# Queries, keys and gates of an encoder block's mixer as pairs of tiles by seven block products, with attention operands stored split and bias and masks as one table

## The chip, the cores and the metric

The kernel runs on one core of one Trainium2 chip. The metric is the device time of one execution in microseconds (us), median of several runs. The profile is one execution of the same program, taken by the hardware profiler.

## The reference

One encoder block over 1024 tokens of width 1024, in float32. The parts that matter here are the projection of the mixer and its two branches:

```python
h = h + 0.5 * swiglu(rms_norm(h, ffn1_norm[i]), ffn1_w_gate[i], ffn1_w_up[i], ffn1_w_down[i])
u = rms_norm(h, mix_norm[i])
z = u @ w_in[i]
q, k, v, s_in, gates = jnp.split(z, splits, axis=-1)      # 512, 512, 512, 512, 2048 columns
y_attn = neighbourhood_attention(q, k, v, na_rpb[i]) @ w_attn_out[i]
y_ssm = s5_branch(s_in, ...) @ w_ssm_out[i]
g_attn, g_ssm = jnp.split(jax.nn.sigmoid(gates), N_BRANCH, axis=-1)
h = h + (g_attn * y_attn + g_ssm * y_ssm) @ w_out[i]
h = h + 0.5 * swiglu(rms_norm(h, ffn2_norm[i]), ffn2_w_gate[i], ffn2_w_up[i], ffn2_w_down[i])
h = h + (p[i] @ ple_w_proj[i]) * jax.nn.sigmoid(rms_norm(h, ple_norm[i]) @ ple_w_gate[i])
return rms_norm(h, final_norm)
```

The attention has 8 heads of 64 over a grid of 16 x 64 tokens; each token sees a window of 8 x 16, with a learned bias by relative place. The state-space branch (S5) runs a complex scan forward and backward for 32 groups of 16 channels, adds a skip, applies GELU and then a gated linear unit: `y * sigmoid(y @ glu_w + glu_b)`.

## The kernel before

All large products are in float32 of two parts: an operand x is stored as xh (rounded) and xl = x - xh, and a product is three passes of TensorE (PE) into one bank of PSUM: xh by wh, xl by wh and xh by wl (`mm3`, lines 184 to 186, of 128x128 by 128x512). The helper `split` (lines 152 to 154) makes the two parts, xh by a copy on ScalarE (ACT) and xl by a subtraction on VectorE (DVE).

Both feed-forward stages already compute their matrices by blocks of two by two with seven products in place of eight: `b_operand` makes the weight side of such a product by sums of blocks on DVE, and A7, ACC7 and NEW7 are the lists of the seven activation operands, of the banks that they add to, and of whether a product begins that bank. The mixer before does not: `proj` (L1037) computes one tile of 128 output columns by 512 tokens as 8 products, each of three passes.

PE's program order is the order in which the code is written. The stage of the mixer, from `sin` (the S5 input, at 684 us) to the last gate tile (1168 us), has one main sequence: S5 input, values, then for four pairs of heads q and k, with the 16 gate tiles (`gt`, L1360) among and behind them. Beside it runs a generator, `mixer_side` (L1286): after every three passes `tick` counts down, and when the count is out the generator advances by one piece of work and yields the number of ticks until the next. Its pieces are the normalisation of the tokens' second half, the injection of the S5 inputs into the scan buffer X, the scan on GpSimd (POOL, L1088), 64 units of attention (8 heads, two row halves, four column blocks), the S5 outputs, and the GLU. `drain` empties what is left of the generator at once.

One unit of attention is, in three calls that lag behind one another, scores (two matmuls, bias and mask, exponential), a transposition, and the products with the values. Its operands stand in SBUF: `qk_proj` writes q and k from PSUM split; `load_v` reads a block of v from DRAM and splits it; `make_tabs` adds bias, row masks and column masks on DVE.

The S5 output of one of 16 pairs of groups (`ssm_out`, L1097) loads two matrices and the inputs by SP, copies the states out of X (`xs`, L1111), has 12 small matmuls on PE (`yo`, L1117 and L1119) and stores the result to y_d in DRAM. From unit 48 of the attention on, each unit is followed by one pair. The GLU reads y_d back in another layout (`yt`, 32 DMAs, L1255), applies GELU, splits, loads its weights (`wgs`, L1269) and computes 8 tiles of 4 products (`glu`), with gate products between. Each engine works through its own queue in order, and so does SP, which issues most of the DMAs. What stands behind a waiting DMA there waits too.

Behind the mixer come the branch products (`br`), which read the attention's and the GLU's outputs from DRAM, the product with w_out, the second feed-forward and the embedding.

## Time and profile before

| | |
|---|---|
| time, median of 3 runs | 2099.38 us (2097.23 to 2100.48) |
| span of the profiled execution | 2094.5 us |
| DMA | 285.19 MB moved, 136 GB/s mean over the span |
| HBM | 201.01 MB read, 82.31 MB written |

The profiled execution is one of its own, measured by the span between its first and last instruction; the runs are timed from outside. The page lists busy time for each engine, the chain of work that ended last, and groups of instructions by line. Answers on tiles give duration (least, median and greatest) and first and last start of all instructions with one name; rows of windows give busy times of the engines in a stretch.

### The profile page before, as it was taken

To read this page: it belongs to the slowest core of one execution; us is meant where nothing else is said; L and a number is where in the kernel's file an instruction comes from. 1 tells how busy PE (TensorE), PEld (TensorE's weight loads), DVE (VectorE), ACT (ScalarE), POOL (GpSimd) and SP (SyncE) were. 2 spreads that over 40 slices of the span, in tenths; PEclk is the share of its full clock that TensorE was granted. 3 is DMA by queue.
4 is the path that set the end of the run, shared out by engine and by line. 5 is a ranking of instruction groups with operands and counts; after the bars stand their busy time and mean duration, and the time that the engine had idled before them with its cause. 6 is when DMAs were issued, how large, how long until landed. Compare 5 with 4: busy or idle time off the path is not lost.

```text
span 2094.5 us, 28063 instructions
## 1 busy us (share of the span) xinstructions
PE 2074.5 (99%) x9662; PEld 1705.4 (81%) x9662; DVE 1416.1 (68%) x2420; ACT 999.6 (48%) x1832; POOL 399.4 (19%) x636
## 2 busy tenths in 40 slices
PE   8999999999999999999999999999999999999998
PEld 3788888888888888888898888788888888888886
DVE  7897776667967334677753668995665665786855
ACT  6434333334445333667774635643333334445543
POOL 0037556441000006888200001000000000000000
PEclk9999999999999999999999999999999999999999
DMA  3435444475533551233477745243324238433302
GB/s 134 143 118 154 125 135 120 144 270 169 188 114 111 159 189 64 70 97 98 123 208 260 247 145 117 77 150 121 100 86 135 82 121 297 155 106 94 118 21 81
DMA packets 197744, 285.19 MB, mean 136 GB/s; under 512 B 41569, under 2 KB 81121, under 8 KB 197601
## 3 DMA queue, kind: packets, MB, share of 16 engines
q1 hardware_dynamic: 180304, 258.20, 38.8%
q10 hardware_dynamic: 14992, 21.00, 3.0%
q0 software_dynamic: 2304, 4.20, 1.2%
q8 instruction: 76, 1.25, 0.2%
q14 instruction: 68, 0.55, 0.1%
HBM read 201.01 MB, written 82.31 MB: 135 GB/s over the span
## 4 chain that ended last, share of the span: by engine, by line
PE 94%; DVE 2%; ACT 1%; DMA 1%; SPq 0%; issue 0%; DVEq 0%; ACTq 0%
PE dx L184 4%; PE dx L185 4%; PE dx L186 4%; PE gx L184 3%; PE ux L184 3%; PE ux L186 3%; PE gx L186 3%; PE gx L185 3%; PE ux L185 3%; PE gt L184 3%; PE gt L185 3%; PE gt L186 3%; PE dy L186 2%; PE dy L184 2%; PE dy L185 2%; PE gy L184 2%
## 5 line engine op out<-in xcount | busy, mean ns | idle before, releaser
L153 ACT CAST wh<-hbuf 128x512 fp32r<-128x512 f32 x280 | 173.0, 622 | 392.3 <-PE gx L185 80.9
L154 DVE TENSOR_TENSOR wl<-hbuf,wh 128x512 fp32r<-128x512 f32 x280 | 209.2, 750 | 122.7 <-ACT wh L153 120.5
L153 ACT CAST wh<-wblk 128x512 fp32r<-128x512 f32 x190 | 118.0, 622 | 192.6 <-PE dx L185 83.2
L154 DVE TENSOR_TENSOR wl<-wblk,wh 128x512 fp32r<-128x512 f32 x190 | 130.6, 690 | 49.3 <-ACT wh L153 41.8
L184 PE MATMUL dx<-ah,wh 128*128 128x512 f32 x416 | 163.3, 393 | 0.3 <-DVE hbuf L688 0.3
L186 PE MATMUL dx<-ah,wl 128*128 128x512 f32 x416 | 161.9, 389 | 0.0
L185 PE MATMUL dx<-al,wh 128*128 128x512 f32 x416 | 161.8, 389 | 0.0
L1092 POOL TENSOR_TENSOR sc<-X,rho 128x128 f32<-128x128 f32 x128 | 77.9, 609 | 327.2 <-ACT X L1075 317.3
L154 DVE TENSOR_TENSOR al<-araw,ah 128x512 fp32r<-128x512 f32 x154 | 106.3, 694 | 50.1 <-PE dx L185 21.1
L184 PE MATMUL gx<-xh,wh 128*128 128x512 f32 x320 | 124.9, 390 | 1.2 <-DVE c L575 1.2
L184 PE MATMUL ux<-xh,wh 128*128 128x512 f32 x320 | 125.0, 390 | 0.0
L186 PE MATMUL ux<-xh,wl 128*128 128x512 f32 x320 | 124.5, 389 | 0.0
L185 PE MATMUL gx<-xl,wh 128*128 128x512 f32 x320 | 124.5, 389 | 0.0
L186 PE MATMUL gx<-xh,wl 128*128 128x512 f32 x320 | 124.5, 389 | 0.0
L185 PE MATMUL ux<-xl,wh 128*128 128x512 f32 x320 | 124.5, 389 | 0.0
L153 ACT CAST ah<-araw 128x512 fp32r<-128x512 f32 x154 | 94.9, 619 | 43.2 <-PE dx L185 12.6
L184 PE MATMUL gt<-xh,wh 128*128 128x512 f32 x256 | 102.7, 401 | 0.0
L186 PE MATMUL gt<-xh,wl 128*128 128x512 f32 x256 | 99.8, 390 | 0.0
L185 PE MATMUL gt<-xl,wh 128*128 128x512 f32 x256 | 99.8, 390 | 0.0
L422 DVE TENSOR_TENSOR hbuf<-hbuf 128x512 f32<-128x512 f32 x120 | 91.4, 762 | 2.1
L184 PEld LDWEIGHTS dx<-ah,wh 128*128 128x128 f32 x416 | 78.1, 188 | 17.8 <-issue 0.7
L185 PEld LDWEIGHTS dx<-al,wh 128*128 128x128 f32 x416 | 78.1, 188 | 16.9 <-issue 0.7
(381 smaller groups left out, 5590.2 us busy)
## 6 DMA issues: line engine op xcount, KB each, us to landing
araw<-a_d SPq DMA_DIRECT2D x154, 256.0 KB
a_d<-c SPq DMA_DIRECT2D x148, 256.0 KB
wblk<-in_wd SPq DMA_DIRECT2D x88, 256.0 KB
hbuf<-in_wg SPq DMA_DIRECT2D x40, 512.0 KB
hbuf<-in_wu SPq DMA_DIRECT2D x40, 512.0 KB
wst<-in_win SPq DMA_DIRECT2D x26, 512.0 KB
hbuf<-in_xT SPq DMA_DIRECT2D x32, 256.0 KB
h_d<-hbuf ACTq DMA_DIRECT2D x32, 256.0 KB
```

The costliest lines, as they stand in the source:

```text
L153: A.copy(hi, src)
L154: return eng.tensor_tensor(lo, src, hi.bitcast(F32), ALU.subtract)
L184: T.matmul(o, lhsT=wh, rhs=xh, start=first, stop=False, skip_group_check=more)
L185: T.matmul(o, lhsT=wh, rhs=xl, start=False, stop=False, skip_group_check=more)
L186: T.matmul(o, lhsT=wl, rhs=xh, start=False, stop=last, skip_group_check=more)
L422: V.tensor_tensor(b11, (b12, b22, None, None, b21)[i - 2], b11, ALU.subtract)
L1092: G.tensor_tensor(sc, both, rho4, ALU.mult)
```

## The change

The mixer's q, k and gate columns are taken in 12 pairs of tiles: for a head pair m the q tile and the k tile (`qk`), and for the gates tiles 2m and 2m+1 (`g`). Each pair of tiles, 256 columns by 1024 tokens, is computed by seven block products as in the feed-forward, with banks `px`, `py` and `pz`. For this the normalised tokens are kept as ten block operands (`U`: a11 to a22 and the sums s1 to s4, made in `u_second` by sums on POOL; s3 goes by DRAM, s_d). Weights are loaded 5 block products ahead and prepared 2 ahead (`s_ahead`).

q and k are split as they leave PSUM and stored to DRAM (q_d, k_d), v too (v_d is twice as wide). `load_k`, `load_q` and `load_v` read them for each head; the second matmul of the scores takes 64 rows. The bias with its masks is gathered on the host as `tabs`, and `load_tab` reads a part for each unit that needs one. The pools of the stage are other: one of 22 buffers of 128x512 ("m"), three of 4 KB a partition ("k4") and 12 of 128x384 ("a").

In `mixer_side` the turn of a unit lags by 2 and its values by 4 (before 3 and 5). The S5 outputs stand behind all 64 units, not beside the last 16, as a loop over pairs that loads two pairs ahead; the GLU follows, in two halves of the tokens: each half has 32 reads of y_d, holds four banks and takes the weights anew. The value of `n` at which `drain` is called is six block products before the last.

```diff
 KNC = (24, 32, 32, 24)
 KVAR = (0, 1, 1, 2)
-KF0 = (8, 0, 0, 0)
+TN = (24, 32, 24)
+TF0 = (8, 0, 0)
+TOFF = (0, 288, 672)
+TABS = 960
...
     a1_d = dtile("a1_d", [NF // 2, 7, P, HT])
     a2_d = dtile("a2_d", [NF // 2, 7, P, HT])
     h2_d = dtile("h2_d", [P, NK * SEQ])
-    v_d = dtile("v_d", [SEQ, 512])
+    v_d = dtile("v_d", [SEQ, 1024])
+    q_d = dtile("q_d", [4, 2, P, SEQ])
+    k_d = dtile("k_d", [4, 2, P, SEQ])
+    s_d = dtile("s_d", [4, P, HT])
     o_d = dtile("o_d", [512, SEQ])
     g_d = dtile("g_d", [16, P, SEQ])
     y_d = dtile("y_d", [NPD, P, NCH])
...
-    u, done, u_first, u_second = halves(h, 1, store_h)
+    U = {name: [] for name in ("a21",) + A7}
+    un = [Norm(h, 0), Norm(h, 1)]
+
+    def done(m, t):
+        un[t].add(m)
+        store_h(m, t)
+
+    def u_put(name, src):
+        hi, lo = tx("xh"), tx("xl")
+        split(hi, lo, src)
+        U[name].append((hi, lo))
```

```diff
 
     win = I["win"]
+    NM = 22
     ap_cm = tc.tile_pool(name="ap", bufs=1, reuse_waits="tile")
     ap_ = ap_cm.__enter__()
-    cur.update(st=(ap_, "st", 3), w=(ap_, "w", 12), tmp=(ap_, "tmp", 4))
...
-            mm3(o, w[k], u[t][k], k == 0, k == NK - 1)
+            mm3(o, w[k], U[("a11", "a12", "a21", "a22")[2 * t + k // 4]][k % 4], k == 0, k == NK - 1)
             tick()
         return o
 
-
...
+    def u_second():
+        yield 10
+        un[1].stat()
+        yield 1
+        for k in range(4):
+            u_norm(k, 1)
+            yield 1
+            u_norm(4 + k, 1)
+            G.tensor_tensor(h[4 + k][1], h[k][1], h[4 + k][1], ALU.add)
+            s3 = tmp("s3")
+            G.tensor_tensor(s3, h[k][0], h[k][1], ALU.subtract)
+            nc.scalar.dma_start(s_d[k], s3)
+            yield 1
+        for k in range(4):
+            u_put("s1", h[4 + k][1])
+            G.tensor_tensor(h[4 + k][1], h[4 + k][1], h[k][0], ALU.subtract)
+            yield 1
+        for k in range(4):
+            u_put("s2", h[4 + k][1])
+            G.tensor_tensor(h[4 + k][0], h[4 + k][0], h[4 + k][1], ALU.subtract)
+            yield 1
+        for k in range(4):
+            u_put("s4", h[4 + k][0])
+            yield 1
...
-        ut = thid("ut", [P, 2, NCH], F32)
+        ut = ta("ut", [P, 2, NCH])
         nc.sync.dma_start(ut, u_d[2 * pr:2 * pr + 2].rearrange("g p c -> p g c"))
         return ut
 
     def inject_load(pr):
-        fm = thid("fmi", [P, HT], F32)
-        nc.sync.dma_start(fm, f_d[pr])
+        fm = [ta("fmi", [P, 256]) for _ in range(2)]
+        for d in range(2):
+            nc.sync.dma_start(fm[d], f_d[pr, :, d * 256:(d + 1) * 256])
...
-    def ssm_out(pr):
-
+    def ssm_load(pr):
         ms = []
         for g in range(2):
-            em = thid("emi", [P, 4, NCH], F32)
-            nc.sync.dma_start(em[:, 0:3].rearrange("p a b -> p (a b)"), e_d[2 * pr + g])
-            nc.sync.dma_start(em[:, 3], u_d[2 * pr + g])
-            ms.append(em)
-
-        xs = tw("xs", [P, 2, 2, NCH], F32)
+            em = ta("emi")
+            nc.sync.dma_start(em, e_d[2 * pr + g])
+            ms.append(em.rearrange("p (a b) -> p a b", a=3))
+        return ms, load_u(pr)
+
+    def ssm_out(pr, ms, ut):
+
+        xs = tmp("xs", [P, 2, 2, NCH])
         for g in range(2):
             for r in range(2):
-                s0 = Xv[g * 64:(g + 1) * 64, r, pr, 0:1]
+                s0 = X["v"][g * 64:(g + 1) * 64, r, pr, 0:1]
                 both = bass.AP(tensor=s0.tensor, offset=s0.offset, ap=[list(s0.ap[0]), [NCH + 2, 2], [1, NCH]])
...
         return go
```

```diff
+    khs, qs, vld, tabs = {}, {}, {}, {}
+    kl_ = {}
+
+    def load_k(hd):
+        hp, i = hd // 2, hd % 2
+        ds = slice(i * 64, (i + 1) * 64)
+        if not kl_:
+            kl_["t"] = ap_.tile([P, SEQ], F32R, tag="k4", bufs=3, name="kl")
+        kh = khs[hd] = ap_.tile([P, SEQ], F32R, tag="k4", bufs=3, name="kh")
+        for s_ in (slice(0, 64), slice(64, P)):
+            nc.sync.dma_start(kh[s_].bitcast(F32), k_d[hp, 0, ds])
+        nc.sync.dma_start(kl_["t"][ds].bitcast(F32), k_d[hp, 1, ds])
+
+    def load_q(hd, rb):
+        hp, i = hd // 2, hd % 2
+        ds, other = slice(i * 64, (i + 1) * 64), slice((1 - i) * 64, (2 - i) * 64)
+        q = qs[hd, rb] = tmp("qs", dt=F32R)
+        nc.sync.dma_start(q[ds].bitcast(F32), q_d[hp, 0, ds, hsl(rb)])
+        nc.sync.dma_start(q[other].bitcast(F32), q_d[hp, 1, ds, hsl(rb)])
 
     def load_v(hd, cb):
         n = 4 * KNC[cb]
-        vf = tmp("vf", [P, 4, 64])
+        hl = tmp("vhl", [P, 4, 2 * 64], F32R)
         for g in range(4):
-            nc.sync.dma_start(vf[0:n, g],
-                              vdr[4 * g:4 * g + 4, KC0[cb]:KC0[cb] + KNC[cb], hd * 64:(hd + 1) * 64])
...
+            nc.sync.dma_start(hl[0:n, g].bitcast(F32),
+                              vdr[4 * g:4 * g + 4, KC0[cb]:KC0[cb] + KNC[cb], hd * 128:(hd + 1) * 128])
...
+    def load_tab(b, v):
         if b < 2 * NH:
-            e0 = 4 - 4 * (b % 2)
...
     def attn_scores(hd, rb, cb):
-        q, kh, kl = qkv[hd]
+        ds = slice((hd % 2) * 64, (hd % 2 + 1) * 64)
         n = KNC[cb]
         nk = 12 * n
-        qv = q[:, rb * HT + cb * P:rb * HT + (cb + 1) * P]
+        q = qs[hd, rb][:, ksl(cb)]
 
...
-        sm = thid("sm", [P, 384], F32)[:, 0:nk]
+        T.matmul(s3, lhsT=q, rhs=kv(khs[hd]), start=True, stop=False)
+        T.matmul(s3, lhsT=q[ds], rhs=kv(kl_["t"])[ds], start=False, stop=True)
+        sm = ta("sm")[:, 0:nk]
+        tab = tabs[2 * hd + rb, KVAR[cb]]
```

```diff
-        glu["x"] = []
+    ygs = {}
+
+    def glu_load(t):
...
+            yt = ygs[t, m] = tmp("yt")
+            yv = yt.rearrange("p (t c) -> p t c", t=4)
+            for g in range(8):
+                nc.sync.dma_start(yv[g * 16:(g + 1) * 16], ydr[8 * m + g][:, 4 * t:4 * t + 4])
+
+    def glu_act(t):
+        for m in range(4):
+            A.activation(ygs[t, m], ygs[t, m], AF.Gelu_apprx_tanh)
+
+    def glu_w(k):
+        w = ap_.tile([P, 2, HT], F32R, tag="k4", bufs=3, name="wgl")
+        raw = tmp("wgs")
+        nc.sync.dma_start(raw, I["wglu"][k])
+        split(w[:, 0], w[:, 1], raw)
+        return w
+
+    def glu_half(t):
+        os_ = [bank("glu") for _ in range(4)]
         for k in range(4):
-            mm3(o, (wm[0][:, ksl(k)], wm[1][:, ksl(k)]), glu["x"][k], k == 0, k == 3)
-        sg = tmp("sg")
-        A.activation(sg, o, AF.Sigmoid, bias=glub[:, m:m + 1])
-        V.tensor_tensor(sg, sg, glu[m][:, hsl(t)], ALU.mult)
-        nc.scalar.dma_start(y2_d[ksl(m), hsl(t)], sg)
-
-    stored = set()
+            w = glu_w(k)
+            y = tmp("yh", dt=F32R), tmp("yl", dt=F32R)
+            split(*y, ygs[t, k])
+            yield 2
+            for m in range(4):
+                mm3(os_[m], (w[:, 0, ksl(m)], w[:, 1, ksl(m)]), y, k == 0, k == 3)
+        for m in range(4):
+            sg = tmp("sg")
+            A.activation(sg, os_[m], AF.Sigmoid, bias=glub[:, m:m + 1])
+            V.tensor_tensor(sg, sg, ygs.pop((t, m)), ALU.mult)
+            nc.scalar.dma_start(y2_d[ksl(m), hsl(t)], sg)
+        yield 2
+
+    stored, ready = set(), set()
+    SO = 56
```

```diff
+                b = 2 * hd + rb
+                load_tab(b + cb // 2, (1, 2, 0, 0)[cb]) if cb < 3 else None
+                if cb == 1 and rb == 0:
+                    load_q(hd, 1)
...
-            if 0 <= j - 3 < n:
-                pts[j - 3] = attn_turn(units[j - 3][2], sms.pop(j - 3))
-            if 0 <= j - 5 < n:
-                hd, rb, cb = units[j - 5]
+            if 0 <= j - 2 < n:
+                pts[j - 2] = attn_turn(units[j - 2][2], sms.pop(j - 2))
+            if 0 <= j - 4 < n:
...
                 if rb == 1 and hd + 1 < NH:
                     load_v(hd + 1, cb)
...
-            yield 4 if j < SO else 3
-        yield 4
+            yield 4
+        scan_steps(NCH)
+        DL = 3
+        for p in range(NPAIR + DL):
+            if p == 0:
+                for q in range(2):
+                    lo[q] = ssm_load(q)
+            if p + 2 < NPAIR:
+                lo[p + 2] = ssm_load(p + 2)
+            if p < NPAIR:
+                so[p] = ssm_out(p, *lo.pop(p))
+            if 0 <= p - 1 < NPAIR:
+                so.pop(p - 1)()
+            yield 2
+        yield 3
+        glu_load(0)
+        yield 5
+        glu_act(0)
+        glu_load(1)
+        yield 2
+        glu_act(1)
+        for t in range(2):
+            yield from glu_half(t)
+
...
+    pairs = [("qk", 0), ("qk", 1), ("g", 0), ("qk", 2), ("g", 1), ("qk", 3)] + [("g", m) for m in range(2, 8)]
+    items = [(n, i) for n in range(len(pairs)) for i in range(7)]
+    sblk, smade, sacc, sz = {}, {}, {}, {}
+
...
+    def s_run(n, i):
+        hi, lo = smade.pop((n, i))
+        a = ACC7[i]
+        if NEW7[i]:
+            sacc[a] = bank("p" + a.lower())
+        for k in range(4):
+            mm3(sacc[a], (hi[:, ksl(k)], lo[:, ksl(k)]), U[A7[i]][k], NEW7[i] and k == 0, k == 3, not NEW7[i])
+            tick()
+        with tc.high_priority(offset=PRI):
+            s_evac(n, i)
+        if i == 6 and pairs[n][0] == "qk":
...
+    oy, W0 = [[], []], []
+    for n, item in enumerate(items):
+        s_ahead(n + 1)
...
+        if n == len(items) - 6:
+            drain()
+            oy[0].append(load_br(0, 0))
+        if n == len(items) - 5:
+            W0.append(load_was(0))
+            W0.append(load_was(1))
+        if n == len(items) - 4:
+            oy[0].append(load_br(0, 1))
+        if n == len(items) - 3:
+            oy[1].append(load_br(1, 0))
+        if n == len(items) - 2:
+            oy[1].append(load_br(1, 1))
+        s_run(*item)
```

Three places in the engines' queues show what the code does. The first is PE at the last S5 pair: `yo` are its matmuls from the inputs (`ut`; before they lie in `emi`), the matrices `emi` and the states `xs`; `glu` are the GLU's products, `gt` gate products, `O` attention's outputs. Before:

```order
L1235 MATMUL O_10891<-pth_10795,vhl_10432 128x128
L1237 MATMUL O_10891<-ptl_10796,vhl_10432 64x128
L1117 MATMUL yo_10898<-emi_10752 128x128
L1119 MATMUL yo_10898<-xs_10758,emi_10752 128x128 x2
L1117 MATMUL yo_10898<-emi_10755 128x128
L1119 MATMUL yo_10898<-xs_10758,emi_10755 128x128 x2
L184 MATMUL gt_10876<-xh_6262,wh_10392 128x512
L185 MATMUL gt_10876<-xl_6263,wh_10392 128x512
L186 MATMUL gt_10876<-xh_6262,wl_10393 128x512
L184 MATMUL gt_10876<-xh_6271,wh_10392 128x512
```

And with the change:

```order
L1181 MATMUL yo_11436<-ut_11389,emi_11385 128x128
L1183 MATMUL yo_11436<-xs_11421,emi_11385 128x128 x2
L1181 MATMUL yo_11436<-ut_11389,emi_11387 128x128
L1183 MATMUL yo_11436<-xs_11421,emi_11387 128x128 x2
L190 MATMUL glu_11526<-yh_11535,wgl_11530 128x512
L191 MATMUL glu_11526<-yl_11536,wgl_11530 128x512
L192 MATMUL glu_11526<-yh_11535,wgl_11530 128x512
L190 MATMUL glu_11527<-yh_11535,wgl_11530 128x512
```

Before, a pair stands between a unit of attention and gate products; now the last pair is followed by the GLU's products at once, as it is preceded by the pair before it.

The second place is SP's queue around the reads of the GLU's inputs (`yt`): `emi` and `ut` are the S5 outputs' loads, `wgs` the GLU's weights, `hbuf` the residual, `g_d` stores of gates and `br` loads of the branch products. Before:

```order
L1102 DMA emi<-e_d 128x384
L1103 DMA emi<-u_d 128x128
L1255 DMA yt<-y_d 16x8x128 x2
L1269 DMA wgs<-in_wglu 128x512
L1255 DMA yt<-y_d 16x8x128 x4
L1364 DMA g_d<-gs 128x512
L1255 DMA yt<-y_d 16x8x128
L1269 DMA wgs<-in_wglu 128x512
L1255 DMA yt<-y_d 16x8x128 x6
L1269 DMA wgs<-in_wglu 128x512 x2
```

And with the change:

```order
L1164 DMA emi<-e_d 128x384 x2
L1118 DMA ut<-u_d 128x2x128
L1601 DMA hbuf<-h_d 128x512 x5
L1283 DMA yt<-y_d 16x4x128 x64
L1292 DMA wgs<-in_wglu 128x512
L1601 DMA hbuf<-h_d 128x512
L1292 DMA wgs<-in_wglu 128x512
L1601 DMA hbuf<-h_d 128x512 x10
L1292 DMA wgs<-in_wglu 128x512 x6
L1457 DMA br<-o_d 128x2x512 x2
```

Before, the reads stood in groups among the weights; now 64 reads of half the size stand in one row ahead of the first weight and behind five loads of the residual.

The third place is ACT's queue at the GLU: `yt` is GELU, `yh` and `wgl` are the first part of the two splits, `sg` the sigmoid. With the change:

```order
L159 CAST yh<-yt 128x512
L159 CAST wgl<-wgs 128x512
L159 CAST yh<-yt 128x512
L159 CAST wgl<-wgs 128x512 x2
L159 CAST yh<-yt 128x512
L1307 ACT_TABLE_LOAD
L1307 ACTIVATE sg<-glu,glub 128x512 x2
L1309 DMA y_d<-sg 128x512
L1307 ACTIVATE sg<-glu,glub 128x512 x2
L1309 DMA y_d<-sg 128x512
L159 CAST yh<-yt 128x512
```

The first split of the second half's inputs stands behind the sigmoids of the first half; before, all splits of one half stood together ahead of its first product.

More of the change, by code (lines that the diff above doesn't have):

```diff
@@ L1292, in mixer_side @@
+    stored, ready = set(), set()
+    SO = 56
+    def mixer_side():
+        yield from u_second()
+        while 1 not in stored:
+            yield 1
+        yield 4
+        new_x()
         ld = {}
@@ L1385, in encoder_block @@
[L1385 to L1386 removed]
+            yield 4
+        scan_steps(NCH)
[11 more added lines that the diff above has]
+            yield 2
@@ new lines, in mixer_side, with load_wv @@
+        yield 3
+        glu_load(0)
+        yield 5
+        glu_act(0)
+        glu_load(1)
+        yield 2
+        glu_act(1)
+        for t in range(2):
+            yield from glu_half(t)
+    start(mixer_side())
+    W = [loadh(win[12 + m], "hid", "hid") for m in range(2)]
+    W += [loadh(win[14 + m], "tmp", "w") for m in range(2)]
+    Wv = []
+    def load_wv(k):
+        st = tmp("wvs")
+        nc.sync.dma_start(st, I["wv"][k // 2][:, hsl(k % 2)])
+        if k < 3:
+            w = ap_.tile([P, 2, HT], F32R, tag="k4", bufs=3, name="wv4")
+            hi, lo = w[:, 0], w[:, 1]
+        else:
+            hi, lo = tw("wvh", [P, HT]), tw("wvl", [P, HT])
+        split(hi, lo, st)
+        Wv.append((hi, lo))
@@ L1387, in encoder_block, with value @@
+    while len(Wv) < NK:
+        load_wv(len(Wv))
+    def value(tt):
         o = bank("v")
@@ new lines, in s_prep, with s_out, view @@
+    def s_prep(n, i):
+        smade[n, i] = b_operand(sblk[n], i)
+    def s_out(n, c, t, second, src):
+        kind, m = pairs[n]
+        if kind == "g":
+            if c == "21":
+                z, src = tmp("z21"), src
+                A.copy(z, src)
+                src = z
+            (nc.scalar if c == "21" else nc.sync).dma_start(g_d[2 * m + second, :, hsl(t)], src)
+            return
+        hi, lo = tmp("qkh", dt=F32R), tmp("qkl", dt=F32R)
+        if second:
+            A.activation(hi, src, AF.Copy, scale=0.125)
+            V.scalar_tensor_tensor(lo, src, 0.125, hi.bitcast(F32), ALU.mult, ALU.subtract)
+        else:
+            def view(x):
+                return x.rearrange("p (b r c) -> p r b c", b=4, r=8)
+            sv = src.rearrange("p (r b c) -> p r b c", r=8, b=4)
+            A.copy(view(hi), sv)
+            V.tensor_tensor(view(lo), sv, view(hi).bitcast(F32), ALU.subtract)
+        for i, x in enumerate((hi, lo)):
+            nc.scalar.dma_start((k_d if second else q_d)[m, i, :, hsl(t)], x.bitcast(F32))
@@ new lines, in s_evac @@
+    def s_evac(n, i):
+        o = sacc
+        z = sz.setdefault(n, {})
+        if i in (0, 2, 3):
+            c, a = (("11", "Z"), None, ("22", "Y"), ("12", "X"))[i]
+            z[c] = tmp("z" + c)
+            A.copy(z[c], o[a])
+            return
+        c, a = {1: ("11", "X"), 4: ("12", "Y"), 5: ("22", "X"), 6: ("21", "X")}[i]
+        if c != "21":
+            V.tensor_tensor(z[c], o[a], z[c], ALU.add)
+        s_out(n, c, int(c[0]) - 1, int(c[1]) - 1, o[a] if c == "21" else z.pop(c))
@@ new lines, in s_run @@
+    def s_run(n, i):
[6 more added lines that the diff above has]
+            tick()
+        with tc.high_priority(offset=PRI):
+            s_evac(n, i)
+        if i == 6 and pairs[n][0] == "qk":
+            ready.update((2 * pairs[n][1], 2 * pairs[n][1] + 1))
+    LL, LP = 5, 2
@@ new lines, in encoder_block, with s_ahead @@
+    done_ = {"l": 0, "p": 0}
+    def s_ahead(n):
+        while done_["l"] < min(len(items), n + LL):
+            s_load(*items[done_["l"]])
+            done_["l"] += 1
+        while done_["p"] < min(len(items), n + LP):
+            s_prep(*items[done_["p"]])
+            done_["p"] += 1
+    for tt in range(NK):
+        if tt == 4:
+            s_ahead(-2)
+        if tt == 6:
+            s_ahead(0)
+        value(tt)
+    s3s = []
+    for k in range(4):
+        s3 = tmp("s3")
+        nc.sync.dma_start(s3, s_d[k])
+        s3s.append(s3)
```

305 lines of the change are left out of this document (103 added, 202 removed).

## The prediction

> **What bounds the kernel now.** I read the page first: its busy times, then the chain that ended last.
>
> ```profile
> span 2094.5 us, 28063 instructions
> PE 2074.5 (99%) x9662; PEld 1705.4 (81%) x9662; DVE 1416.1 (68%) x2420; ACT 999.6 (48%) x1832; POOL 399.4 (19%) x636
> PE 94%; DVE 2%; ACT 1%; DMA 1%; SPq 0%; issue 0%; DVEq 0%; ACTq 0%
> ```
>
> TensorE (PE) works 99% of the span and holds 94% of the chain. A product that goes is therefore worth its full spacing on PE, as long as nothing else becomes late; and whatever lets PE stand idle is paid in full. The span is 2094.5 us, the median of the runs 2099.38 us: 4.9 us lie around the span, and I carry them over. The windows (PE, weight loads, DVE, ACT, POOL busy, granted clock, DMA share, GB/s) say the same of the mixer, from its first product at 684 us to its last at 1168 us:
>
> ```profile
> 684.00:1168.00 484.00, 482.77 (x2659) 414.94 (x2658) 259.86 (x568) 273.65 (x560) 181.91 (x384) 1.00 0.46 141
> 1029.00:1101.00 72.00, 70.93 (x495) 64.16 (x494) 39.98 (x112) 52.60 (x125) 0.00 (x0) 1.00 0.71 207
> 1040.00:1060.00 20.00, 19.99 (x139) 18.04 (x139) 13.85 (x43) 16.31 (x43) 0.00 (x0) 1.00 0.76 226
> 2084.00:2094.00 10.00, 0.70 (x2) 0.30 (x2) 5.55 (x11) 1.81 (x5) 0.00 (x0) 0.68 0.55 184
> ```
>
> Of 484 us PE rests 1.2. The second row is the stretch in which the SSM outputs run, one pair of groups for each attention unit: there PE rests 1.1 us of 72, since gate products stand between. The third row is that stretch's busiest part for DMA: 226 GB/s at a share of 0.76, so by my estimate 226/0.76 = 297 GB/s when the queues are full.
>
> **Removed: 144 products.** Gate, query and key products each take three passes:
>
> ```profile
> L184 PE MATMUL gt<-xh,wh x256: 387/389/481, 695.7 to 1167.3; 128*128 128x512 f32 x128
> L184 PE MATMUL q<-xh,wh x64: 389/389/448, 808.7 to 996.1; 128*128 128x512 f32 x64
> L184 PE MATMUL k<-xh,wh x64: 389/389/448, 819.5 to 1011.6; 128*128 128x512 f32 x64
> 1104.99 0.40 PE L185 MATMUL gt<-xl,wh 128*128 128x512 f32 x1
> ...
> 1122.90 0.39 PE L186 MATMUL gt<-xh,wl 128*128 128x512 f32 x1
> ```
>
> (256 + 64 + 64) x 3 = 1152 products go; 12 pairs x 7 block products x 4 x 3 = 1008 come. The duration of 389 ns is not the price, for products overlap: from the first to the last timeline row lie 79 products in 17.91 us, 0.2267 us each. 144 x 0.2267 = **-32.6 us**. The order of PE has exactly 144 rows less, so that the change would not do what it says is no rival.
>
> **Moved: the SSM outputs and the GLU.** The side work advances one step per three products; with 48 steps fewer, the 64 attention units only just end before the forced emptying, six block products before the end. All 16 output pairs and the whole GLU then stand on PE in one piece, with no gate product between. What hid their waits is gone.
>
> *The pairs.* What a pair costs PE and what it moves:
>
> ```profile
> 1080.29 0.43 PE L1117 MATMUL yo<-emi 128*128 128x128 f32 x2
> 1080.56 0.61 PE L1119 MATMUL yo<-xs,emi 128*128 128x128 f32 x4
> 1081.00 0.39 PE L1117 MATMUL yo<-emi 128*128 128x128 f32 x2
> 1081.23 0.61 PE L1119 MATMUL yo<-xs,emi 128*128 128x128 f32 x4
> L1119 PE MATMUL yo<-xs,emi x128: 275/275/275, 1029.2 to 1099.5; 128*128 128x128 f32 x128
> emi<-e_d SPq DMA_DIRECT2D x32, 192.0 KB
> ut<-u_d SPq DMA_DIRECT2D x16, 128.0 KB
> y_d<-ys ACTq DMA_DIRECT2D x16, 128.0 KB
> ```
>
> The first six products of a pair take from 1080.29 to 1081.00, 0.71 us; so a pair is 1.42 us and 16 pairs 22.7 us of PE, as before. Per pair, two loads of 192 KB, one of 128 KB and a store of 128 KB are 655 KB (1024 bytes to a KB), at 297 GB/s 2.2 us: more than PE's 1.42. Only four pairs have room (12 slots, three a pair), so twelve loads follow at that pace: 26.5 us, and with the first slot's return (3.7 us from issue to use, the weight row below) and two pairs of PE (2.8) 33 us. Against 22.7 that is **+10.3 us**. Bounds: 0 if loads keep PE fed as before; +18.6 at the 226 GB/s that the window shows (655/226 = 2.9 us a pair, 12 of them 34.8).
>
> *From the last pair to the first GLU product.* The GLU's inputs are read from DRAM by SP (SyncE's queue), whose order is: the last pair's load, 5 residual loads that wait for the scan buffer to come free, 64 reads of 16x4x128 (before: 32 of 16x8x128), then the first GLU weight.
>
> ```profile
> L1255 SPq DMA_DIRECT2D yt<-y_d x32: 302/430/1461, 1072.6 to 1112.7; - x32
> 1084.64 0.43 SPq L1103 DMA_DIRECT2D emi<-u_d  x1
> 1096.11 0.40 SPq L1269 DMA_DIRECT2D wgs<-in_wglu  x1
> 1105.08 5.13 SPq L1255 DMA_DIRECT2D yt<-y_d  x10
> 1111.73 1.40 SPq L1255 DMA_DIRECT2D yt<-y_d  x3
> 1099.85 0.62 ACT L153 CAST wgh<-wgs 128x512 fp32r<-128x512 f32 x1 [1.48 <-DMA wgs<-in_wglu]
> L154 DVE TENSOR_TENSOR al<-araw,ah 128x512 fp32r<-128x512 f32 x154 | 106.3, 694 | 50.1 <-PE dx L185 21.1
> ```
>
> The trace shows no read of the new, half as large shape. One read takes SP 0.43 us (median), in series 1.40/3 = 0.47 and 5.13/10 = 0.51. I take 0.45: 64 x 0.45 = 28.8 us. Before these, 5 loads x 0.43 = 2.1; behind them, weight issue to use 1099.85 - 1096.11 = 3.7, and its two splits 0.62 + 0.69 = 1.3. Together 35.9. SP can begin about 4.4 us before the last pair's last product (the last copies that read the scan buffer stand two pairs ahead of it, 2 x 2.2), so PE stands idle for 35.9 - 4.4 = **+31.5 us**. Bounds from the row's ends: at its fastest, 0.33 (near the 302 ns minimum), 21.1 + 7.1 - 4.4 = 24; at 0.565 with waits (1.1 times the longer series), 36.2 + 7.1 - 4.4 = 39. Before, this cost nothing: from the last pair at 1099.5 to the GLU at 1123.1 PE had gate products.
>
> *Inside the GLU.* Its 96 products take 21.8 us as before:
>
> ```profile
> L184 PE MATMUL glu<-yh,wgh x32: 389/389/389, 1123.1 to 1156.5; 128*128 128x512 f32 x32
> 1154.61 0.69 ACT L1280 ACTIVATE sg<-glu,glub 128x512 f32<-128x512 f32 x1 [1.98 <-PE glu L186]
> ```
>
> It now runs in two halves with four banks, each half reading the weights again. ACT has the first half's four sigmoids (4 x 0.69 = 2.76) ahead of the second half's first split (0.62, then 0.69 on DVE): 4.1 us, some 4.5 with the hand-overs. The third weight stands behind 10 residual loads on SP: about 2 us. **+6.5 us**; bounds 0 (all prepared ahead) and +11 (every one of the remaining weights late by some 0.75 us more). Behind the GLU, 72 block products (16.3 us) and the first half of the branch products (48, 10.9 us) cover its way through DRAM: nothing.
>
> **Stored split and gathered tables.** The DVE work that goes (table sums) was not on PE's path: DVE is busy 260 of 484 us. What comes is waits: first scores behind keys that go through DRAM (issue to use 3.7 us, mostly scanned over by other products), the side sums of the second half on POOL, lookahead of two units in place of three, and SP with 16 value reads a head as before:
>
> ```profile
> L1167 SPq DMA_DIRECT2D vf<-v_d x128: 509/610/1117, 807.5 to 1077.8; - x128
> L1092 POOL TENSOR_TENSOR sc<-X,rho 128x128 f32<-128x128 f32 x128 | 77.9, 609 | 327.2 <-ACT X L1075 317.3
> ```
>
> A unit is issued every 12 block products, 2.72 us; 16 reads x 0.61 = 9.8 us a head fit in the eight units of a head (21.8 us). I take **+3 us** for all seams; bounds 0 and +12 (a round trip of 3.7 at three starts). POOL, where the scan runs, has 0.00 us left in the window of the outputs, so the scan is done ahead of them and I leave it at nothing.
>
> **Sum.** 2094.5 - 32.6 + 10.3 + 31.5 + 6.5 + 3 = 2113.2; with 4.9 around it **2118 us**. All low ends: 2094.5 - 32.6 + 24 + 4.9 = 2091. All high ends: 2094.5 - 32.6 + 18.6 + 39 + 11 + 12 + 4.9 = 2147.
>
> The clock after the idle stretch is the place where a page differs from this sum. In the last window PE works 0.70 of 10 us and the granted clock is 0.68; elsewhere it is 1.00. I leave the sum at 1.00, as the GLU's 22 us have little rest in them. The Trainium skill, "TensorE: Matmul & The Clock Gate", Part 1 (The HAM clock gate), says that after an idle window of about 3.4 us the clock is half and comes back after as long a busy one. By that rule the first 3.4 us of GLU products would run at half speed: an estimate of 1.7 us more, 2120. The row of 0.68 agrees with a lower clock in rest; how fast it comes back, no row here shows.
>
> **Rivals.**
>
> *Faster (the other side).* The reads issue at 0.33 us and all else of the tail is hidden: the pairs at PE's pace, weights ready. Then the hole is 24 us and the time 2091 us. The point where it turns: the four terms behind the -32.6 must sum to under 32.6; with the pairs, GLU and seams at 0, the hole must be under that, and 64 c + 2.7 < 32.6 gives c < 0.47 us per read. For it: reads of half the size, and minima of 302 ns. Against it: both series at 0.47 and above, and the full load on DMA in the pairs.
>
> *Even.* Fast reads (24), but the pairs at DMA's pace (+10.3): 2094.5 - 32.6 + 34.3 + 4.9 = 2101; or reads at 0.45 with everything else hidden (31.5), 2098.
>
> *The loop starves.* 22 slots now serve weights, evacuations and attention's inputs, and the lookahead is shorter: 0.4 us lost on each of 64 units, 26 us more: 2144. Against it: DVE and ACT are busy 260 and 274 of the mixer's 484 us.
>
> *Slow clock.* The GLU's 96 products at 0.68 throughout: 21.8/0.68 = 32.0, +10.2: 2129.
>
> **Chances.** Forecast 0.60 (its own range 2104 to 2134); faster 0.15; even 0.12; starving 0.08; slow clock 0.05. The forecast is the likeliest. The range 2090 to 2136 leaves out half of the faster case, the starving one and a rest of the forecast, about 0.2. A measurement of this kernel can tell about 0.2% (4 us) from no change: faster 0.15, same 0.12, slower 0.73.
>
> **What would show it.** 144 products fewer; the pairs in about 33 us instead of 70, with PE idle between them on their loads; one idle stretch of some 30 us before the first GLU product while SP issues 64 reads; rest at the halves' boundary; a clock below 1.00 in the hole; the mixer near 504 us in place of 484. If reads issue under 0.4 us each, or the GLU reads were ahead of the pairs' end, the forecast falls; if block products wait for operands all along the loop, the starving case holds.

## The result, and the profile after

The changed kernel takes 2195.53 us (median of 3 runs, 2193.82 to 2197.26) against 2099.38: the ratio is 1.0463, with a 95% interval of 1.0444 to 1.0482. It is slower, as forecast, but by 96 us where 19 were forecast, and outside the range of 2090 to 2136.

The page of the changed kernel, its span, its busy times and the chain of work that ended last:

```profile
span 2192.0 us, 28396 instructions
PE 2089.9 (95%) x9518; PEld 1684.9 (77%) x9518; DVE 1465.8 (67%) x2470; ACT 1015.1 (46%) x1870; POOL 436.4 (20%) x652
PE 85%; DVE 6%; DMA 3%; SPq 2%; ACT 2%; issue 1%; POOL 0%; ACTq 0%; DVEq 0%
```

PE has 144 matmuls fewer, and yet is busy for 15 us more. Its share of the chain falls from 94% to 85%; DVE, DMA, SP's queue and ACT take its place. The next view has the mixer by stretches (us; busy time and count of PE, weight loads, DVE, ACT, POOL; granted clock, DMA share, GB/s). The first two rows run to the values' end, one is from the loop of attention, then follow the pairs of the S5 outputs, the stretch up to the GLU, the GLU, the last block products, and the branch products:

```profile
700.00:740.00 40.00, 33.38 (x138) 25.87 (x137) 35.46 (x34) 18.23 (x29) 25.90 (x16) 0.91 0.40 97
740.00:810.00 70.00, 62.18 (x319) 52.00 (x318) 23.15 (x47) 20.24 (x46) 4.78 (x13) 0.93 0.67 174
...
1000.00:1100.00 100.00, 97.38 (x526) 75.87 (x525) 58.31 (x142) 60.18 (x136) 22.14 (x45) 1.00 0.56 164
...
1139.40:1176.30 36.90, 26.14 (x194) 24.03 (x192) 10.71 (x35) 19.49 (x49) 0.00 (x0) 0.95 0.84 254
1176.30:1210.00 33.70, 0.10 (x2) 0.05 (x1) 0.76 (x2) 7.81 (x12) 0.00 (x0) 0.56 0.35 105
1210.00:1244.80 34.80, 28.42 (x97) 21.44 (x98) 13.72 (x21) 13.94 (x23) 0.00 (x0) 0.84 0.56 180
1244.80:1266.00 21.20, 18.48 (x74) 14.52 (x73) 14.23 (x21) 11.76 (x19) 0.00 (x0) 0.92 1.03 275
1266.00:1360.00 94.00, 94.00 (x417) 77.82 (x416) 62.21 (x94) 50.55 (x83) 6.24 (x7) 1.00 0.63 203
1360.00:2192.00 832.00, 820.51 (x3660) 678.00 (x3658) 575.79 (x914) 372.17 (x631) 7.90 (x9) 1.00 0.36 115
```

From the first branch product to the end the kernel takes 926.1 us, where it took 926.5 before: there nothing changed. All the loss lies between 684 and 1266 us, 582 us in place of 484. PE does nearly nothing in one stretch of 33.7 us. The second view is what PE waited for in the whole span (total us, times, longest):

```profile
PE glu L190 <- ACT wgl L159: 39.5, 3, 33.6
PE px L190 <- DVE z L1535: 11.2, 11, 2.4
PE yo L1181 <- DMA ut<-u_d: 8.1, 9, 2.1
PE py L190 <- ACT z L1531: 6.3, 2, 6.0
PE v L1439 <- ACT wvh L159: 6.1, 2, 3.6
PE sin L191 <- DVE xl L160: 5.0, 4, 2.6
```

These six are 76 us, and half of them is the GLU. The forecast idle stretch is there, and its cause can be read on two engines' timelines. First SP's (start, length, instruction):

```profile
1175.94 30.44 SPq L1283 DMA_DIRECT2D yt<-y_d  x64
```

Then PE's, with the idle time before the instruction and what ended it:

```profile
1209.95 0.80 PE L190 MATMUL glu<-yh,wgl 128*128 128x512 f32 x1 [33.60 <-ACT wgl L159]
```

SP takes 30.44 us for 64 reads, 0.476 us each, then the first weight can be loaded. PE's last pair ends at 1176.3.

**A ledger.** The spans differ by 97.5 us. If the removed products are worth 32.6 us as forecast, 130.1 us were added. The tail holds 65.8 of these: the pairs 36.9 - 22.7 = 14.2, the idle stretch 33.7, the GLU 34.8 - 21.8 = 13.0, and the 72 last block products 21.2 - 16.3 = 4.9. The other 64.3 came earlier, where the prediction had 3. The experiments looked for those.

### The profile page after: what moved, and what is told of

Same layout as the page of the kernel before. It is cut to its first block, busy times and chain, and to the rows that moved or that the text cites. A ratio compares the mean times of both kernels' runs of the same rounds, so it can differ in the third digit from the quotient of the medians.

```text
span 2192.0 us, 28396 instructions
## 1 busy us (share of the span) xinstructions
PE 2089.9 (95%) x9518; PEld 1684.9 (77%) x9518; DVE 1465.8 (67%) x2470; ACT 1015.1 (46%) x1870; POOL 436.4 (20%) x652
## 4 chain that ended last, share of the span: by engine, by line
PE 85%; DVE 6%; DMA 3%; SPq 2%; ACT 2%; issue 1%; POOL 0%; ACTq 0%; DVEq 0%
PE dx L190 4%; PE dx L191 4%; PE dx L192 4%; PE gx L190 3%; PE ux L190 3%; PE gx L192 3%; PE ux L192 3%; PE ux L191 3%; PE gx L191 3%; PE dy L191 2%; PE dy L192 2%; PE dy L190 2%; PE px L190 2%; PE px L191 2%; PE px L192 2%; PE gy L190 2%
## 5 line engine op out<-in xcount | busy, mean ns | idle before, releaser
L160 DVE TENSOR_TENSOR al<-araw,ah 128x512 fp32r<-128x512 f32 x154 | 106.1, 693 | 51.8 <-PE dx L191 21.2
L159 ACT CAST ah<-araw 128x512 fp32r<-128x512 f32 x154 | 94.9, 619 | 47.1 <-PE dx L191 14.2
L190 PEld LDWEIGHTS dx<-ah,wh 128*128 128x128 f32 x416 | 78.1, 188 | 18.6 <-DVE hbuf L694 1.2
L192 PEld LDWEIGHTS dx<-ah,wl 128*128 128x128 f32 x416 | 78.1, 188 | 16.3
L190 PE MATMUL px<-xh,wh 128*128 128x512 f32 x192 | 78.8, 410 | 12.1 <-DVE z L1535 11.2
L421 POOL DMA_DIRECT2D wblk<-in_wout x16 | 14.1, 934 | 339.5 <-ACT wblk L420 339.2
```

Source lines behind the costliest of these rows:

```text
L159: A.copy(hi, src)
L160: return eng.tensor_tensor(lo, src, hi.bitcast(F32), ALU.subtract)
L190: T.matmul(o, lhsT=wh, rhs=xh, start=first, stop=False, skip_group_check=more)
L192: T.matmul(o, lhsT=wl, rhs=xh, start=False, stop=last, skip_group_check=more)
L421: G.dma_start(blk[i], src, accum_op=ALU.add)
```

## The experiments

Each ran beside the kernel before on the same chip; medians there lie between 2098.2 and 2099.0 us. Ratios are to these. What an edit of the changed kernel wins is counted from its 2195.53 us, which three runs on another occasion gave with a spread of 3.4 us; gains of 7 to 9 us are rough by that much.

**Scores on 64 rows.** In the changed kernel the second scores product takes 64 rows of the array. PE's timeline there shows 1.40 us for a unit that took 1.05. The same edit alone in the kernel before:

```diff
+        ds = slice((hd % 2) * 64, (hd % 2 + 1) * 64)
-        T.matmul(s3, lhsT=qv, rhs=kv(kl), start=False, stop=True)
+        T.matmul(s3, lhsT=qv[ds], rhs=kv(kl)[ds], start=False, stop=True)
```

> The kernel before, with its second scores product on the head's 64 rows alone (the product of q's low part with k's low part is left out). Theory: PE pays for each change between a matmul on 64 rows and one on 128. After the change a unit takes PE 1.40 us from its scores to the next block product, before it 1.05 us, so 64 units cost 64 x 0.35 = 22 us. Expected: PE's unit 1.40 us and about 2122 us. Rival: the longer unit comes from something else in the changed stage (operands read from other buffers, DMA at work). Then this run stays within 4 us of 2099, its unit at 1.05 us.

2118.48 us, ratio 1.0096 (1.0081 to 1.0111): 20.3 us more, 0.32 us for each unit. PE's timeline of one unit in the kernel before:

```profile
1002.71 0.29 PE L1207 MATMUL s<-kh,qs 128*128 128x288 f32 x1
1002.83 0.30 PE L1208 MATMUL s<-kl,qs 128*128 128x288 f32 x1
1002.97 0.49 PE L1223 MATMUL pt<-ident,sm 128*128 128x128 f32 x3
...
1003.76 0.44 PE L184 MATMUL k<-xh,wh 128*128 128x512 f32 x1
```

And in this run (behind the names stand the array's rows x columns, then the operand's shape):

```profile
1002.02 0.29 PE L1207 MATMUL s<-kh,qs 128*128 128x288 f32 x1
1002.24 0.40 PE L1209 MATMUL s<-kl,qs 64*128 64x288 f32 x1
1002.57 0.55 PE L1224 MATMUL pt<-ident,sm 128*128 128x128 f32 x3
...
1003.42 0.45 PE L184 MATMUL q<-xh,wh 128*128 128x512 f32 x1
```

The matmul on 64 rows starts 0.22 us behind the one ahead in place of 0.12, and what follows starts 0.33 us behind it in place of 0.14. Nothing is shown as a wait: PE counts as busy. The price of the theory holds, and its rival falls. Whether PE pays for the change of rows or for the narrow matmul itself is not shown, as no run has two such matmuls in a row.

The other way round, with 128 rows in the changed kernel:

```diff
-            kl_["t"] = ap_.tile([P, SEQ], F32R, tag="k4", bufs=3, name="kl")
+        kl = kl_[hd] = ap_.tile([P, SEQ], F32R, tag="k4", bufs=4, name="kl")
...
-        nc.sync.dma_start(kl_["t"][ds].bitcast(F32), k_d[hp, 1, ds])
+        for s_ in (slice(0, 64), slice(64, P)):
+            nc.sync.dma_start(kl[s_].bitcast(F32), k_d[hp, 1, ds])
...
-        T.matmul(s3, lhsT=q[ds], rhs=kv(kl_["t"])[ds], start=False, stop=True)
+        T.matmul(s3, lhsT=q, rhs=kv(kl_[hd]), start=False, stop=True)
...
-    NM = 22
+    NM = 20
```

> The changed kernel, with the low part of k loaded for each head into both halves of the rows, so that the second scores product takes 128 rows again (one more buffer of 4 KB, two fewer of 2 KB, one more load a head). Theory of the 64 rows: the unit falls from 1.40 to 1.05 us, about 2173 us. Rival (operands or DMA): about 2195 us. If the two fewer buffers hurt, more than 2195.

2193.81 us, ratio 1.0452 (1.0436 to 1.0468): no gain in the time. But on PE's timeline the unit takes 1.07 us again:

```profile
1020.40 0.29 PE L1234 MATMUL s<-kh,qs 128*128 128x288 f32 x1
1020.53 0.29 PE L1235 MATMUL s<-kl,qs 128*128 128x288 f32 x1
...
1021.47 0.44 PE L190 MATMUL py<-xh,wh 128*128 128x512 f32 x1
```

And the answer on the tile O (duration least, median, greatest; first and last start) has the last unit's last product at 1117.6 us, where the changed kernel has it at 1137.2:

```profile
L1262 PE MATMUL O<-pth,vhl x192: 220/276/307, 863.1 to 1117.6; 96*128 96x128 f32 x96, 128*128 128x128 f32 x96
```

Twenty us were won there and given back in the GLU, whose weights now wait for buffers. SP's waits in that run name who holds them, the sigmoid's product and the GLU's own products:

```profile
SPq L1292 <- DVE sg L1308: 12.9, 1, 12.9
SPq L1292 <- PE glu L191: 12.1, 3, 4.7
```

To tell the buffers from the rest of that edit, the two buffers alone were taken away (`NM = 20`, nothing else):

> The changed kernel with 20 buffers of 128x512 in place of 22, nothing else. Theory: with 128 rows the units fell by 20 us but the GLU's span grew from 35 to 56 us, because each weight waits for a buffer that the products before it hold; the two buffers alone do this. Expected: the GLU's span 50 to 57 us again and about 2214 us. Rival: the fourth 4 KB buffer or the added loads did it; then this run stays within 5 us of 2195.

2216.91 us, ratio 1.0562 (1.0547 to 1.0578): 21.4 us more than the changed kernel. The GLU's first passes start from 1214.2 to 1270.1 us here, and from 1210.0 to 1244.0 in the changed kernel. The answers on the tile, first of this run:

```profile
L190 PE MATMUL glu<-yh,wgl x32: 389/628/795, 1214.2 to 1270.1; 128*128 128x512 f32 x32
```

And of the changed kernel:

```profile
L190 PE MATMUL glu<-yh,wgl x32: 389/393/796, 1210.0 to 1244.0; 128*128 128x512 f32 x32
```

So both amounts, 20 us for the rows and 21 for two buffers, are shown apart.

**The sums on POOL.** Four calls in `u_second`:

```diff
-            G.tensor_tensor(h[4 + k][1], h[k][1], h[4 + k][1], ALU.add)
+            V.tensor_tensor(h[4 + k][1], h[k][1], h[4 + k][1], ALU.add)
...
-            G.tensor_tensor(s3, h[k][0], h[k][1], ALU.subtract)
+            V.tensor_tensor(s3, h[k][0], h[k][1], ALU.subtract)
...
```

> The changed kernel with the 16 block sums of the tokens on DVE in place of POOL. Theory: at 700 to 735 us DVE's operations take 1.13 and 1.33 us instead of 0.75 and 0.69 because POOL works beside them, and PE's 5.0 us of waits for xl and part of the low clock there follow from it. Expected: the operations at 0.69 to 0.75 us again, PE's waits for xl under 2 us, time 4 to 8 us less, about 2189. Rival: DVE is the bound with or without POOL (16 sums are 11 us more of its own); then the operations are short but the time stays within 3 us of 2195.

2183.36 us, ratio 1.0404 (1.0387 to 1.0421): 12.2 us less, above what was expected. In the changed kernel the groups of a split on DVE (count, total us, mean ns) and of a sum on POOL are these:

```profile
L160 DVE TENSOR_TENSOR xl<-hbuf,xh 128x512 fp32r<-128x512 f32 x20 | 25.4, 1334 | 0.0
```

```profile
L1093 POOL TENSOR_TENSOR hbuf<-hbuf 128x512 f32<-128x512 f32 x4 | 6.9, 1740 | 0.0
```

In this run both are on DVE:

```profile
L160 DVE TENSOR_TENSOR xl<-hbuf,xh 128x512 fp32r<-128x512 f32 x20 | 13.0, 679 | 0.0
L1093 DVE TENSOR_TENSOR hbuf<-hbuf 128x512 f32<-128x512 f32 x4 | 2.6, 679 | 0.0
```

Beside POOL the subtraction of a split takes twice its time; without it DVE does the 16 sums as well and is done earlier. PE's wait for xl falls from 5.0 to 1.2 us.

**Value reads in one piece.** Right behind the first keys stand 16 value reads, and behind them the weights of the next block products:

```diff
+            if "v" in stored and ev < 4 and wait % 5 == 0:
+                load_v(0, ev)
+                ev += 1
...
-        for cb in range(4):
+        for cb in range(ev, 4):
             load_v(0, cb)
```

> The changed kernel with the first head's 16 value reads issued one group at a time while the first block products run, not all at once behind the first keys. Theory: these 16 reads hold SP for 12.4 us, and the block weights behind them are what PE waits 6.0 us for at 847 us. Expected: that wait gone, 5 to 6 us less, about 2190. Rival: the weights are late for another reason (slots); then the wait stays and the time is 2195.

2188.56 us, ratio 1.0428 (1.0412 to 1.0444): 7.0 us less. In the changed kernel SP's timeline has the 16 reads:

```profile
833.38 12.38 SPq L1215 DMA_DIRECT2D vhl<-v_d  x16
```

And PE's has the wait behind them:

```profile
847.24 0.79 PE L190 MATMUL py<-xh,wh 128*128 128x512 f32 x1 [6.04 <-ACT z L1531]
```

In this run the longest wait of PE between 820 and 870 us is 1.0 us. The releaser named, a copy on ACT, had itself stood behind a split of weights that came late.

**Value weights behind stores.** The load of each value weight goes ahead of the eight stores of the S5 input, not behind them:

```diff
-            if t == 0 or m > 1:
-                load_wv(len(Wv))
+            if t == 0 and m == 0:
+                load_wv(0)
             o = proj(W[m], t, "sin")
...
+            if len(Wv) < 4 or t == 1 and len(Wv) < NK:
+                load_wv(len(Wv))
             for g in range(8):
```

> The changed kernel with each load of value weights issued ahead of the eight stores of the S5 inputs, not behind them. Theory: with the sums on DVE 12 of the 24 us lost up to the values went; the rest is PE waiting for value weights (6.1 us named, and a clock of 0.51 beside it at 750 to 760), whose load stands behind stores that wait for ACT's copies. Expected: the waits for wvh under 1 us, 6 to 9 us less, about 2188. Rival: the weights wait for buffers or for ACT; the waits stay and the time is within 3 us of 2195.

2186.74 us, ratio 1.0418 (1.0402 to 1.0433): 8.8 us less. No wait for wvh is left, and the first block product starts 6.3 us earlier (802.9 in place of 809.2).

The last three edits (sums, value reads, value weights) win 28.0 us together, but the waits that they end are only 3.8 + 6.0 + 6.1 = 15.9. The granted clock accounts for a part of the difference. Two stretches of the changed kernel with such waits (columns as in the rows of windows above):

```profile
710.00:720.00 10.00, 6.01 (x16) 4.00 (x17) 10.00 (x10) 2.47 (x4) 7.51 (x5) 0.66 0.25 65
750.00:760.00 10.00, 5.54 (x15) 3.76 (x16) 2.08 (x3) 1.82 (x3) 0.00 (x0) 0.51 0.67 206
```

The clock falls at these waits and stays low for some us behind them; passes then start 0.43 us apart in place of 0.23. Each edit raises it in its own stretch: from 0.91 to 1.00 at 700 to 740 us with the sums on DVE, from 0.94 to 1.00 at 810 to 863 with early value reads, from 0.93 to 0.98 at 740 to 810 with the new order of the value weights.

**The tail's reads.** Half of the 64 reads of the GLU's inputs issued by ACT:

```diff
-                nc.sync.dma_start(yv[g * 16:(g + 1) * 16], ydr[8 * m + g][:, 4 * t:4 * t + 4])
+                (nc.scalar if g % 2 else nc.sync).dma_start(yv[g * 16:(g + 1) * 16], ydr[8 * m + g][:, 4 * t:4 * t + 4])
```

> The changed kernel with every second read of the GLU's inputs issued by ACT in place of SP. Theory: the idle stretch before the GLU is the issue of 64 reads on one queue (30.4 us for 64); on two queues it falls by 12 to 15 us, to about 2182 us. Rival: the reads land no faster because the transfers themselves or their slots bound them; then the stretch stays at 33 us and the time at 2195.

2180.25 us, ratio 1.0393 (1.0377 to 1.0410): 15.3 us less. SP's timeline:

```profile
1175.09 18.98 SPq L1283 DMA_DIRECT2D yt<-y_d  x32
```

And PE's waits for the GLU's weights (total, times, longest):

```profile
PE glu L190 <- ACT wgl L159: 28.5, 3, 23.6
```

The longest wait falls by 10.0 us, from 33.6 to 23.6, short of the 12 to 15 expected: the idle stretch is mostly SP's issue, though the reads on two queues take 0.59 us each on SP. Another 4.1 us are won behind it, in the GLU and the last block products.

**The tail beside block products.** Shorter waits in `mixer_side`, reads of y_d behind the pairs that write them, weights two ahead, and the emptying later:

```diff
-            yield 4
+            yield 3
         scan_steps(NCH)
...
-            yield 2
-        yield 3
-        glu_load(0)
+            yield 3
+            if p >= 6 and (p - 6) % 4 == 0:
+                for t in range(2):
+                    glu_load(t, (p - 6) // 4)
...
+            glu_prep(4 * t + k + 2)
...
-        if n == len(items) - 6:
+        if n == len(items) - 3:
             drain()
```

> The changed kernel with its tail beside block products again: a unit of attention is due after 3 steps in place of 4, the S5 outputs after 3, the reads of the GLU's inputs stand behind the pairs that they read from, GLU weights are prepared two ahead, and the emptying comes three block products before the end instead of six. Theory: the tail costs cover alone, 33.7 us before the GLU, 13 in it, 14 in the pairs and 5 behind; most of it goes, 55 to 60 us: about 2138 us, with no idle stretch of PE over 3 us there. Rival: the loop is limited by SP, ACT and DVE, so that what is won at the tail comes back as waits of block products: 2165 us or more.

2161.23 us, ratio 1.0296 (1.0279 to 1.0313): 34.3 us less, short of the 55 to 60, though under the rival's 2165. One idle stretch of 12.1 us remains ahead of the GLU, as the last 30 reads, 15.63 us on SP, and the weights behind them still come late.

**The same fault in the kernel before.** One number, and the loop's end that follows from it:

```diff
-        SO = 48
-        for j in range(n + 6):
+        SO = 64
+        for j in range(n + 22):
```

> The kernel before with nothing changed but the unit of attention from which the S5 outputs begin: 64 in place of 48. The last five pairs and the whole GLU then stand on PE without gate products between, as all pairs and the GLU do in the changed kernel. Theory of the cover: PE stands idle while SP issues 32 reads of 0.45 to 0.53 us (14 to 17 us) and for 3 to 5 us of table, GELU and splits behind them, and 2 to 4 us at the pairs: about 2120 us, between 2116 and 2126. Rival: the loss at the changed kernel's tail comes from its two halves, four banks and single buffers of weights; then this run stays under 2106.

2113.33 us, ratio 1.0066 (1.0051 to 1.0081): 14.5 us more, just below the forecast's 2116 to 2126, above the rival's 2106. SP's timeline has the last reads:

```profile
1142.32 7.09 SPq L1255 DMA_DIRECT2D yt<-y_d  x14
```

And PE's has the wait ahead of the GLU:

```profile
1146.38 0.80 PE L184 MATMUL glu<-yh,wgh 128*128 128x512 f32 x1 [10.82 <-ACT yh L153]
```

With whole tiles, all splits ahead and no change of arithmetic, the uncovered GLU still costs PE 13.1 us of waits at two places. The longer one is not for these last reads, whose issue ends at 1149.4 us. PE waits there for the first input's split, which stands on ACT behind the splits of four weights; the last two of these weights were issued only at 1141.4, as loads of weights had waited 6.9 us on SP for the pairs' stores. Only the second wait, 2.2 us at 1153.3, is for the last reads: SP had issued 16 of the 32 while pairs still ran. So the run shows the price of missing cover, but not the theory's idle time of 14 to 17 us for reads.

**All together.** Four versions of the changed kernel with these edits. The first has the tail beside block products, 128 rows, early value reads and value weights ahead. It has 20 buffers of 128x512 too, and reads the branch products' inputs in smaller pieces. The GLU's inputs lie in four 4 KB buffers that attention leaves, so 32 reads suffice:

```diff
-            yt = ygs[t, m] = tmp("yt")
+        yt = ygs[m] = ap_.tile([P, SEQ], F32, tag="k4", bufs=4, name="yt")
```

> The changed kernel with the causes mended together: tail beside block products (units after 3 steps, pairs after 2), the GLU's inputs as 32 reads into the 4 KB buffers that attention leaves, its weights two ahead, the second scores product on 128 rows, the first head's values early, value weights loaded ahead of the stores of the S5 inputs. By the amounts found so far: 2195.5 - 33.7 (idle before the GLU) - 12 (in it) - 13 (pairs) - 20 (rows) - 6 (values) - 4 (value weights) = about 2107 us. Rival: the loop is bound by buffers (20 of 128x512) and queues at the quicker pace, and waits of block products take the place: 2125 or more.

2135.23 us, ratio 1.0172 (1.0156 to 1.0187): the rival's side, 28 us above the sum. Then with the sums on DVE:

> The combined kernel with the block sums on DVE as well. Theory (the sums' price adds to the others): 12 us off, about 2123 us. Rival: part of it is covered by the value weights' order, which the combined kernel has too: 2128 to 2133.

2126.19 us, ratio 1.0134 (1.0117 to 1.0151): 9.0 us less, between the two. Then with the transposition three units behind:

```diff
-            if 0 <= j - 2 < n:
-                pts[j - 2] = attn_turn(units[j - 2][2], sms.pop(j - 2))
+            if 0 <= j - 3 < n:
+                pts[j - 3] = attn_turn(units[j - 3][2], sms.pop(j - 3))
...
-            yield 3
+            yield 4 if j < 12 else 3
```

> The same with a transposition three units behind its scores in place of two (values stay at four), and units after 4 steps for the first 12, then 3. Theory: in the combined kernel PE waits 5 us for exponentials and 14 us for evacuations of block products because units come every 9 products; with one more unit of slack the first goes and the second shrinks: 2113 to 2120 us. Rival: the slack only moves, the values now wait for the transposed parts, and the later GLU gives back cover: no less than the run with the sums alone.

2118.24 us, ratio 1.0093 (1.0078 to 1.0108), as expected. Last, all units after 3 steps, and 72 products between the pairs and the GLU:

> The combined kernel with sums on DVE, transposition three units behind, all units after 3 steps, and more block products ahead of the GLU (72 between the last pair and its first product) and in it (9 between steps). Theory: in the run before PE stood 18 us idle at the GLU for its inputs and sigmoids, and under a low clock; all of this has cover now: 2098 to 2104 us, as the kernel before, since what is left is the waits of the loop. Rival: units every 9 products wait for ACT and DVE, and the loop gives back what the GLU gains: 2112 or more.

2114.83 us, ratio 1.0084 (1.0066 to 1.0101): the rival's side. The mixer up to its last block product in this run (columns as above):

```profile
684.00:1186.00 502.00, 466.85 (x2520) 393.38 (x2519) 299.84 (x636) 281.81 (x595) 190.79 (x384) 0.99 0.70 206
```

And in the changed kernel:

```profile
684.00:1266.00 582.00, 498.44 (x2521) 395.59 (x2520) 310.04 (x618) 287.44 (x596) 218.26 (x400) 0.94 0.60 174
```

Of the 582 us 80 are gone. PE is busy for 467 us, 16 less than before the change (482.77), though 32.6 us of products are gone, and idle for 35 where it was idle for 1.2. No version here beats the kernel before.

## Why the prediction was wrong

**The removed products.** 144 fewer, and between units block products still start 0.227 us apart. The term stands.

**The tail.** The mechanism was right, but the terms were too small together: pairs +14.2 (forecast 10.3, bound 18.6), idle stretch 33.7 (31.5; 0.476 us a read against 0.45), the GLU 13.0 (6.5, bound 11), and 4.9 behind it where nothing was put. That is 65.8 in place of 48.3. Of the GLU's 13.0 us 6.4 are waits, as forecast, though the wait of 3.9 us between its halves ended with a late weight and not with ACT's sigmoids alone. The other 6.6 us are products at a lower clock (28.4 us busy for 21.8). That cover is the cause is shown from two sides: more of it in the changed kernel, with weights two ahead and the reads moved, wins 34 us; less of it in the kernel before costs 14.5. The row that the prediction calls the busiest for DMA is not (1080 to 1100 us has 233 GB/s at 0.78), which leaves its estimate of 297 GB/s as it is.

**The failed step** is "I take **+3 us** for all seams; bounds 0 and +12". If the removed products are worth 32.6 us, it came to 64. Taken one by one, 20.3 are the passes on 64 rows, 12.2 the sums on POOL, 8.8 the value weights and 7.0 the first value reads; 48.3 together, though these amounts were taken apart and the sums and weights overlap (9.0 in place of 12.2 where the weights were mended first). Of the other 16, PE's waits for evacuations of block products ahead of the tail, 8.7 of the 11.2 us in the view above, are the largest piece that has a name; no run took them alone, and the rest stays open.

**A second step that failed** is "I leave the sum at 1.00, as the GLU's 22 us have little rest in them". Between 684 and 1266 us PE is busy for 33.8 us at a granted clock of 0.50, of which 15.7 lie ahead of the pairs; before the change there was none in the mixer. From the spacing of 0.43 us in place of 0.227 this costs an estimated 16 us. By PE's own time the loss reads so: 82 us more of idle time, and 15.7 us more of busy time with 32.6 us of products gone. These 48 us of slower work are 20 for the 64 rows, some 16 for the clock, and some 12 that stay open.

Three pieces of the seams were in view. The second scores product "takes 64 rows" was described with the change and got no term, and no row of before had a matmul on 64 rows to bound it. "16 reads x 0.61 = 9.8 us a head fit in the eight units" is an average over a head; the first head's 16 stand in one piece, at 0.77 us each, with weights behind them. And POOL's sums were named among the seams, without what POOL does to DVE. The case of a loop that starves, with a chance of 0.08, had 2144, closest of all. That it came closest is luck: of its 26 us for lost slots and lookahead the trace shows 7.0 between 863 and 1139 us, as waits for evacuations.

**The rivals.** The faster case fell: reads took 0.476 us, above its 0.47, and the other terms were not nil. The slow clock came, with 0.84 over the GLU in place of 0.68 (the case's own sum is 2128, not 2129), and in stretches ahead of the pairs too, where no case had it.

**Mending.** The experiments explain where the time went, but do not add up to a gain: with all causes treated PE is still idle for 35 us of the mixer. Of these, 26 us end with DVE or ACT and 8 with a DMA. The same side work now stands beside fewer products, and units closer together wait for DVE and ACT; that this is the reason is argued, not shown.

## What to carry to other kernels

Price a new shape of matmul by measuring it among its neighbours: here an operand on half of the rows cost more than it saved, and showed as busy time, not as a wait. Look at the granted clock behind each new wait: here a wait of a few us cost more than its own length. When products are removed from an engine that covers side work paced by these products, list what side work then stands alone, and price its queue (number of DMAs times issue) and not only its bytes. A gain in one stretch can be given back in another through shared buffers, so compare stretch by stretch, and not the time alone.
